# Taking gathered picks 24 at a time in a tuned two-layer expert kernel

## The chip, the cores and the metric

One core of a Trainium2 chip. The metric is device time in microseconds (us) of one launch; 2041.65 us is the median of three runs before the change (2041.55 to 2047.14).

## The reference

A backbone of two layers for 256 latent and 256 context tokens of width 1024, all in fp32. Layer 1 mixes with state-space heads and latent attention, layer 2 with a chunked gMLP. Each layer ends in a PEER expert block, where the change does most of its work:

```python
s1 = jnp.einsum('thd,hkd->thk', q[..., :half], k1)
s2 = jnp.einsum('thd,hkd->thk', q[..., half:], k2)
v1, i1 = lax.top_k(s1, PEER_TOPK)
v2, i2 = lax.top_k(s2, PEER_TOPK)
...
top_s, j = lax.top_k(cand_s, PEER_TOPK)
idx = jnp.take_along_axis(cand_i, j, axis=-1)
gate = jax.nn.softmax(top_s.astype(jnp.float32), axis=-1).astype(h.dtype)
...
act = jax.nn.gelu(jnp.einsum('phkd,pd->phk', jnp.take(u_tab, ib, axis=0), tb), approximate=False)
return jnp.einsum('phk,phkd->pd', gb * act, jnp.take(v_tab, ib, axis=0))
```

So each of the 256 tokens picks 8 heads × 16 = 128 of 16384 experts, each with a gate; an expert is a row of `u_tab`, against which the token is scored, and a row of `v_tab`, which is added with gate × gelu(score). Every sub-layer is scaled and shifted by a modulation vector, the product of a condition with `ada_w` (1024 × 6144 per layer).

## The kernel before

Every instruction is issued through a wrapper, so nearly all carry the line of that helper, L169 (L173 in the changed kernel), and are told apart by their tiles. The wrapper also books the instruction in a planner (`Clock`) that keeps a planned time per engine. `schedule()` takes several generators and goes on with the one whose engine is least far; a generator yields conditions on the planned times. The order of each engine's queue is fixed so, when the program is built; on the chip each engine runs its queue in order and waits on semaphores.

The expert block, `peer()`, works on two tiles of 128 tokens. A pick's expert number is class × 128 + row. The first X = 75 classes are computed densely, the picks of all others are gathered.

- `stage2(t)` finds the 128 picks of each token and writes the sort key `key[t]`, for gathered picks only, and the gates `gte[t]`.
- First pass: 75 "S units", each of 8 matmuls `pa<-phf,wr` (128x256), for one class, its 512 KB of weights loaded on the SP queue into one of 4 buffers `wr`. `spread()` turns the dense picks' gates into columns by matmuls `pb<-oc,o`, whose operands the vector engine (DVE) builds.
- Second pass: 75 "V units", each of 8 matmuls `pb<-wr,ge`, again 512 KB a unit.
- Beside both passes `gather()` handles the picks of the other classes, one per token at a time. `take8()` takes the eight largest keys of every token: it unpacks the row and the place among the 128 picks, and fetches the gate at that place by eight multiplies `mk` over 128 columns. `fetch()` on POOL loads 128 rows of 8 KB (u and v together) by an indirect DMA into one of NR = 6 buffers `rows`. On DVE `dot()` writes `junk` and the score, and `accumulate()` adds into `acc`.
- Each tile of tokens has CAP = 56 picks of its own gathered so. The up to LEFT = 16 others of a token go to three shared lists of 128. `listing()` counts them (`cnt`, a flag `fl`) on DVE, ranks them by small matmuls on the tensor engine (PE) (`pa<-cnt,tri`, `pa<-cnt,ones`, `pa<-fl,ones`), then by comparisons `cmp` and matmuls `pa<-rhs,cmp`. The lists are fetched (`rows<-in_uv,lidx` with their tokens' vectors `rows<-hs,lidx`) and added by matmuls `pb<-rows,sc` of 512 columns into the second pass's sums.
- `ending()` takes tile 0's `acc` through DRAM (`acs`, written and read on the SP queue, where the weight loads stand too) and adds the input of the layer.
- `overflow()` is a branch for more left-over picks than the lists hold.

The modulation is made by `ada_group()`: pieces of 128 × 512 of `ada_w` come on the SP queue into NAW = 4 buffers `aw`, one matmul `pb<-aw,condT` with 32 output rows each. Its generator runs beside the other work of the hybrid layer.

Of the kernel before, what the change touches and what calls it, by code (L numbers as in the profile page):

```python
# [10 lines left out]
F32 = mybir.dt.float32  # L11
# [3 lines left out]
I32 = mybir.dt.int32  # L15
# [5 lines left out]
P = 128  # L21
# [6 lines left out]
GSC = 32768.0  # L28
ROOM = 36
TB, TL = 8, 4  # L30
CAP = 56
ROUNDS = 9
SHARED = 3
# [16 lines left out]
NAW = 4  # L50
KORDER = (8, 10, 12, 0, 2, 4, 6, 14)
LAG = 2

# [144 lines left out]
def tile_backbone(ctx: ExitStack, tc: tile.TileContext, a: dict, out: bass.AP):  # L198
# [50 lines left out]

    def mm(o, lhsT, rhs, start=True, stop=True):  # L250
        T.matmul(o, lhsT, rhs, start=start, stop=stop)

# [48 lines left out]
    ms = [dp.tile([P, 512], F32, name=f"ms{g}") for g in (1, 2)]  # L301
    LEFT = 8 * ROUNDS - CAP
    lts = dp.tile([2 * P * LEFT, 2], F32, name="lts")

# [1108 lines left out]
    def peer(l, mod, a2, sh2):  # L1413
# [3 lines left out]

        key = [[q1.tile([P, P], F32, name=f"key{t}{i}") for i in range(2)] for t in range(2)]
        iota_i = key[0][0].bitcast(I32)
        G.iota(iota_i, [[1, P]], base=0, channel_multiplier=0)  # L1420
        jp1 = q1.tile([P, P], F32, name="jp1")
        V.tensor_scalar(jp1, iota_i, 1.0, None, op0=ALU.add)
        place_i = q1.tile([P, SHARED], I32, name="place_i")
# [14 lines left out]
        pkT = [q1.tile([P, 4, P], F16, name=f"pkT{t}") for t in range(2)]  # L1438
        gidx = [q1.tile([P, 8 * ROUNDS], I32, name=f"gidx{t}") for t in range(2)]
        gsel = [q1.tile([P, 8 * ROUNDS], F32, name=f"gsel{t}") for t in range(2)]  # L1440
        gte = [q1.tile([P, P], F32, name=f"gte{t}") for t in range(2)]
# [47 lines left out]
        def stage2(t):  # L1489
# [107 lines left out]

        def take8(t, r_, idx=None, gsl=None):

            if idx is None:  # L1600
                idx, gsl = gidx[t][:, 8 * r_:8 * r_ + 8], gsel[t][:, 8 * r_:8 * r_ + 8]
# [3 lines left out]
            ki = q2.tile([P, 8], I32, tag="ki", name="ki")  # L1605
            V.tensor_copy(ki, ks)
            z_ = q2.tile([P, 8], F32, tag="z_", name="z_")
            V.tensor_scalar(z_, ks, 0.0, 65536.0, op0=ALU.is_equal, op1=ALU.mult)
            V.tensor_scalar(idx, ki, 8, None, op0=ALU.logical_shift_right)
            V.tensor_tensor(idx, idx, z_, op=ALU.add)  # L1610
            V.tensor_scalar(ki, ki, 255, None, op0=ALU.bitwise_and)
            j1 = q2.tile([P, 8], F32, tag="j1", name="j1")
            V.tensor_copy(j1, ki)
# [146 lines left out]
        def choose():  # L1760
            wait[0], feed.eager = QWAIT, False
            yield lambda: "q" in done
            wait[0] = GTH
            yield from stage2(0)
            for i, _ in enumerate(stage2(1)):
                if i == 4:
                    turn(0)
                yield
            for r_ in range(EARLY):
                take8(0, r_)  # L1770
# [12 lines left out]
            done.add("G")  # L1783
            todo_v[:] = []
            wait[0] = LAST
# [23 lines left out]
        def listing():  # L1809

            ps = pa()
            rhs = q2.tile([P, 2, 2], F32, tag="rhs", name="rhs", bufs=1)
            V.memset(rhs, 1.0)
            for t in range(2):
                vm = q2.tile([P, LEFT], F32, tag="vm", name="vm")
# [7 lines left out]
                fl = q2.tile([P, 1], F32, tag="fl", name="fl")  # L1823
                V.tensor_reduce(fl, key[t][ROUNDS % 2], axis=AX.X, op=ALU.max)
                V.tensor_scalar(fl, fl, 0.0, None, op0=ALU.is_gt)
                mm(ps[:, t:t + 1], tri, cnt[:, t:t + 1], True, t == 0)
# [3 lines left out]
                mm(ps[:, 3 + 2 * t:4 + 2 * t], ones, fl)  # L1830
# [3 lines left out]
            V.tensor_tensor(ends[:, 2:4], ends[:, 2:4], ps[:, 4:6], op=ALU.add)  # L1834
            ps = pa()
# [26 lines left out]
        def gather():  # L1862
# [7 lines left out]
            def issue():  # L1870
# [4 lines left out]
                if t < 2:  # L1875
                    if s % 8 == 0 and s // 8 >= taken[t]:
                        take8(t, taken[t])
                        taken[t] += 1
# [42 lines left out]
            while work or pend:  # L1921
                weigh_last()
                if work:
# [6 lines left out]
                    if t == 1 and s >= 4:  # L1930

                        if taken[0] < ROUNDS or taken[1] < ROUNDS:
                            t_ = 0 if taken[0] < ROUNDS else 1
                            take8(t_, taken[t_])
                            taken[t_] += 1
                        elif lst is None:
                            lst = listing()
                        if lst:
                            next(lst, None)
                if len(pend) > LAG or not work:  # L1940
                    if len(pend) == 1:
                        weigh_last()
                    if pend[0][0] == 2:
                        yield at(pend[0][3])
                    accumulate()
                while head[0] < len(todo) and len(work) + len(pend) < NR:
                    if todo[head[0]][0] == 2 and todo[head[0]][1] == 0:
                        while taken[0] < ROUNDS or taken[1] < ROUNDS:
                            t_ = 0 if taken[0] < ROUNDS else 1
                            take8(t_, taken[t_])  # L1950
                            taken[t_] += 1
# [34 lines left out]
        def overflow():  # L1986
# [8 lines left out]
            with tc.If(rv > 0):  # L1995
                for t in range(2):
# [3 lines left out]
                    V.tensor_tensor(gsel[t][:, CAP:], gsel[t][:, CAP:], pos, op=ALU.mult)  # L2000
                    for r_ in range(CAP // 8, P // 8):
                        if r_ < ROUNDS:
                            idx, gsl = gidx[t][:, 8 * r_:8 * r_ + 8], gsel[t][:, 8 * r_:8 * r_ + 8]
                        else:
                            idx = q2.tile([P, 8], I32, tag="oidx", name="oidx")
                            gsl = q2.tile([P, 8], F32, tag="ogs", name="ogs")
                            take8(t, r_, idx, gsl)
                        for s in range(max(0, CAP - 8 * r_), 8):
                            rw = qr["rows"][s % NR]
# [121 lines left out]
```

## Time and profile before

| | us |
|---|---|
| median of three runs | 2041.65 |
| the profiled execution | 2042.83 |
| its span in the profile | 2041.0 |
| busy: tensor engine / its weight loads | 1886.9 / 1516.0 |
| busy: vector engine | 1429.6 |
| busy: scalar engine / GpSimd | 545.9 / 630.8 |

The profile is of one execution. PE is the tensor engine, PEld its weight loads, DVE the vector engine, ACT the scalar engine, POOL GpSimd, SP the queue on which the weights are loaded. Matmuls are pipelined and their ends modelled; an fp32 matmul of 128x256 leaves two records, so a unit of 8 leaves 16. A timeline row groups like instructions in a row and gives in brackets the idle time before the first of them and what ended it. 1.8 us of the execution's time lie outside the span.

### The profile page before, as it was taken

How to read it: one execution, taken by the hardware profiler on the slowest of the kernel's cores; microseconds unless marked ns; L12 is line 12 of the kernel's file. 1: busy time of each engine (PE TensorE's matmuls, PEld its weight loads, DVE VectorE, ACT ScalarE, POOL GpSimd, SP SyncE). 2: the span in 40 equal slices, each digit the busy share in tenths (PEclk: the TensorE clock that was granted, in tenths of full speed). 3: DMA queues.
4: the chain of work that ended last, by engine and by line, in shares of the span. 5: the costliest groups of instructions: out<-in, count | busy, mean ns of one | idle time of the engine just before them, and what ended most of it. 6: DMA issues, size and time to landing. Idle time of an engine off the chain costs nothing.

```text
span 2041.0 us, 28033 instructions
## 1 busy us (share of the span) xinstructions
PE 1886.9 (92%) x9728; PEld 1516.0 (74%) x9728; DVE 1429.6 (70%) x3796; ACT 545.9 (27%) x1438; POOL 630.8 (31%) x402
## 2 busy tenths in 40 slices
PE   7899999999989999987999798999899999978997
PEld 3666444479968888876878588789778888867785
DVE  3565576246996888879767526478988888697665
ACT  4434253354212222110111254443122221101111
POOL 2324312176011112232422279551112112224221
PEclk9999999999989999999899899999989999988999
DMA  8555664545366889998899464453578888988993
GB/s 298 181 172 200 225 222 138 190 160 187 129 225 241 286 306 336 351 377 313 316 417 394 175 227 164 140 192 127 188 295 294 325 324 319 366 316 318 417 402 132
DMA packets 133065, 529.87 MB, mean 260 GB/s; under 512 B 17941, under 2 KB 18133, under 8 KB 105197
## 3 DMA queue, kind: packets, MB, share of 16 engines
q1 hardware_dynamic: 97440, 301.76, 41.8%
q0 software_dynamic: 34176, 225.07, 29.1%
q8 instruction: 77, 1.26, 0.3%
q10 hardware_dynamic: 1296, 1.16, 0.2%
q14 instruction: 76, 0.62, 0.1%
HBM read 540.28 MB, written 6.91 MB: 268 GB/s over the span
## 4 chain that ended last, share of the span: by engine, by line
PE 36%; issue 29%; DVE 17%; POOL 12%; ACT 2%; DMA 2%; POOLq 0%; SPq 0%; ACTq 0%; DVEq 0%
PE pa L169 23%; PE pb L169 14%; POOL rows L169 10%; DVE ge L169 6%; POOL whl L169 2%; DVE rows L169 1%; DVE acc L169 1%; DMA rows<-hs,lidx 1%; DVE oc L169 1%; DVE junk L169 1%; DVE mk L169 1%; DVE x L169 1%; DVE o L169 1%; DVE cacc L169 0%; POOLq L169 0%
## 5 line engine op out<-in xcount | busy, mean ns | idle before, releaser
L169 POOL DMA_INDIRECT rows<-in_uv,gidx x224 | 266.8, 1191 | 930.0 <-DVE acc L169 619.9
L169 PE MATMUL pb<-wr,ge 128*128 128x256 f32 x2400 | 542.1, 386 | 13.1 <-DMA wr<-in_dn 11.3
L169 PE MATMUL pa<-phf,wr 128*128 128x256 f32 x2400 | 539.8, 385 | 0.0
L169 PEld LDWEIGHTS pb<-wr,ge 128*128 128x128 f32 x2400 | 458.5, 193 | 96.5 <-DMA wr<-in_dn 32.1
L169 PEld LDWEIGHTS pa<-phf,wr 128*128 128x128 f32 x2400 | 459.8, 193 | 62.0
L169 POOL TENSOR_TENSOR whl<-wr,whl 128x1024 fp32r<-128x1024 f32 (+2 forms) x130 | 314.7, 2434 | 363.6 <-ACT whl L169 337.4
L169 DVE SCALAR_TENSOR_TENSOR junk<-rows,h 128x1024 bf16<-128x1024 f32 x224 | 273.5, 1221 | 99.9 <-DMA rows<-in_uv,gidx 99.7
L169 DVE SCALAR_TENSOR_TENSOR acc<-rows,wt,acc 128x1024 f32<-128x1024 f32 x220 | 281.8, 1281 | 0.0
L169 ACT ACTIVATE act<-act 128x1 f32<-128x1 f32 x230 | 47.0, 204 | 547.3 <-DVE junk L169 531.8
L169 ACT CAST whl<-wr 128x1024 fp32r<-128x1024 f32 (+2 forms) x136 | 136.9, 1019 | 74.5 <-issue 26.4
L169 ACT ACTIVATE sg<-pa 128x256 f32<-128x256 f32 (+25 forms) x116 | 34.4, 296 | 352.4 <-PE pa L169 313.1
L169 PE MATMUL pb<-oc,o 128*128 128x75 f16 x1024 | 85.3, 252 | 28.6 <-DVE oc L169 26.8
L169 PEld LDWEIGHTS <-o 128*128 128x128 f16 x1024 | 78.2, 118 | 38.0 <-DVE o L169 16.5
L169 PE MATMUL pa<-phh,whl 128*128 128x256 f32 x512 | 96.3, 285 | 2.6 <-DVE phf L169 2.2
L169 PE MATMUL pb<-aw,condT 128*32 128x512 f32 x328 | 94.0, 624 | 3.5 <-DVE mod L169 2.7
L169 DVE SCALAR_TENSOR_TENSOR ge<-pb,ge 128x80 f32<-128x80 f32 (+31 forms) x128 | 37.0, 323 | 73.4 <-ACT ge L169 73.2
L169 PEld LDWEIGHTS pa<-phh,whl 128*128 128x128 f32 x512 | 80.8, 191 | 4.7 <-DVE phf L169 2.5
L169 DVE SCALAR_TENSOR_TENSOR mk<-jp,j,gte 128x128 f32<-128x128 f32 x288 | 81.5, 348 | 1.3
L169 PE MATMUL pa<-phl,whl 128*128 128x256 f32 x256 | 73.2, 286 | 2.3 <-POOL phl L169 1.3
L169 ACT ACTIVATE wt<-act,gsel 128x1 f32<-128x1 f32 x224 | 66.0, 295 | 7.3
L169 PE MATMUL pb<-whl,cath 128*128 128x512 f32 x192 | 61.8, 400 | 2.0 <-POOL whl L169 1.2
L169 ACT ACTIVATE ge<-pa 128x256 f32<-128x256 f32 (+24 forms) x136 | 40.2, 296 | 81.4 <-PE pa L169 81.4
(525 smaller groups left out, 2436.2 us busy)
## 6 DMA issues: line engine op xcount, KB each, us to landing
wr<-in_dn SPq DMA_DIRECT2D x300, 512.0 KB, 6.6
aw<-in_ada_w SPq DMA_DIRECT2D x164, 256.0 KB, 3.3
wr<-in_wq SPq DMA_DIRECT2D x32, 512.0 KB, 3.2
wr<-in_w_out SPq DMA_DIRECT2D x16, 512.0 KB, 3.3
wr<-in_gm_w_v SPq DMA_DIRECT2D x16, 512.0 KB, 3.6
wr<-in_gm_w_u SPq DMA_DIRECT2D x16, 512.0 KB, 3.4
wr<-in_gm_w_out SPq DMA_DIRECT2D x16, 512.0 KB, 3.2
wr<-in_w_xbc SPq DMA_DIRECT2D x12, 512.0 KB, 4.8
```

The source lines that it names most:

```text
L169: return f(*args, **kw)
```

## The change

Five edits.

1. `take8` becomes `take`: 24 picks at a time, three takes a tile in place of nine. The gate is no longer looked up: `stage2` makes three keys per tile (5 more operations of 128x128, and 2 products with the mask), all with the place `jd` in their high bits, and the row, the gate's upper and its lower part below. Three MAX8 and three MATCH_REPLACE8 per eight picks sort all three alike. Of the takes before the spread (EARLY) one is left in place of two. The picks now come in the order of their place, not of their expert number.
2. `listing()` does its DVE work first, yields four times, and only then issues its counting matmuls; the comparisons are made at once, and the `rhs,cmp` matmuls follow three yields later.
3. The `sc` matmuls are issued LATE = 6.0 planned us behind the point where their weights are ready.
4. `mm()` issues an fp32 matmul of 512 columns and 128 output rows as two of 256 columns (92 of them in the order).
5. `ada_group()` handles its pieces in pairs: it waits for two, issues their matmuls, and then two loads.

```diff
-ROOM = 36
+ROOM = 38
...
-ROUNDS = 9
+TAKE, TAKES = 24, 3
...
+LATE = 6.0
...
     def mm(o, lhsT, rhs, start=True, stop=True):
+        if rhs.dtype == F32 and lhsT.dtype == F32 and len(rhs.shape) == 2 and rhs.shape[1] == 512 and o.shape[0] == P:
+
+            T.matmul(o[:, :256], lhsT, rhs[:, :256], start=start, stop=False)
+            T.matmul(o[:, 256:], lhsT, rhs[:, 256:], start=False, stop=stop)
+            return
         T.matmul(o, lhsT, rhs, start=start, stop=stop)
...
-        for i in range(len(units) + n - 1):
+        for i in range(0, len(units) + n, 2):
+            if i >= n:
+
+                yield at(*bufs[i % n:i % n + 2])
+                for j in range(2):
+                    k, t = units[i - n + j]
+                    mm(ps[32 * t:32 * t + 32, :], condT[:, k, :], bufs[i % n + j], k == 0, k == KD - 1)
             if i < len(units):
-                k, t = units[i]
-                aw = bufs[i % n]
-                yield lambda: clk["T"] >= clock.idle(aw)
-                Q.dma_start(out=aw, in_=a["ada_w"][l, k * P:(k + 1) * P, g * 2048 + t * 512:g * 2048 + (t + 1) * 512])
-            if i >= n - 1:
-                k, t = units[i - n + 1]
-                aw = bufs[(i - n + 1) % n]
-                yield at(aw)
-                mm(ps[32 * t:32 * t + 32, :], condT[:, k, :], aw, k == 0, k == KD - 1)
+                yield lambda: clk["T"] >= max(clock.idle(x) for x in bufs[i % n:i % n + 2])
+                for j in range(2):
+                    k, t = units[i + j]
+                    Q.dma_start(out=bufs[i % n + j], in_=a["ada_w"][l, k * P:(k + 1) * P, g * 2048 + t * 512:g * 2048 + (t + 1) * 512])
...
-            V.scalar_tensor_tensor(key[t][0], cg, 256.0, jp1, op0=ALU.mult, op1=ALU.add)
+            V.scalar_tensor_tensor(key[t][0], jd, float(ROWS), cg, op0=ALU.mult, op1=ALU.add)
             V.tensor_tensor(key[t][0], key[t][0], mk, op=ALU.mult)
+            yield
+
+            gi = qr["s"].tile([P, P], I32, tag="gi", name="gi")
+            V.tensor_scalar(gi, gte[t], GHI, None, op0=ALU.mult)
+            V.scalar_tensor_tensor(cg, gte[t], GHI, gi, op0=ALU.mult, op1=ALU.subtract)
+            V.scalar_tensor_tensor(key[t][1], jd, 65536.0, gi, op0=ALU.mult, op1=ALU.add)
+            V.tensor_scalar(gi, cg, GLO, 32768.0, op0=ALU.mult, op1=ALU.add)
+            V.scalar_tensor_tensor(key[t][2], jd, 65536.0, gi, op0=ALU.mult, op1=ALU.add)
+            for i in (1, 2):
+                V.tensor_tensor(key[t][i], key[t][i], mk, op=ALU.mult)
...
-        EARLY = 2
+        EARLY = 1
...
-        def take8(t, r_, idx=None, gsl=None):
+        def take(t, r_, idx=None, gsl=None):
...
-            ks = q2.tile([P, 8], F32, tag="ks", name="ks")
-            V.max(ks, key[t][r_ % 2])
-            V.match_replace(key[t][(r_ + 1) % 2], ks, key[t][r_ % 2], 0.0)
...
-            for s_ in range(8):
-                mk = q2.tile([P, P], F32, tag="mk", name="mk")
-                V.scalar_tensor_tensor(mk, jp1, j1[:, s_:s_ + 1], gte[t], op0=ALU.is_equal, op1=ALU.mult, accum_out=gsl[:, s_:s_ + 1])
+            ks = [tmp(f"ks{i}", F32) for i in range(3)]
+            for e in range(0, TAKE, 8):
+                for i in range(3):
+                    V.max(ks[i][:, e:e + 8], key[t][i])
+                for i in range(3):
+                    V.match_replace(key[t][i], ks[i][:, e:e + 8], key[t][i], 0.0)
...
+            V.tensor_scalar(lo, kc, 1.0 / (GLO * GHI), -32768.0 / (GLO * GHI), op0=ALU.mult, op1=ALU.add)
+            V.scalar_tensor_tensor(gsl, kb, 1.0 / GHI, lo, op0=ALU.mult, op1=ALU.add)
+            V.tensor_tensor(gsl, gsl, ok, op=ALU.mult)
...
+            for _ in range(4):
+                yield
+            ps = pa()
+            for t in range(2):
                 mm(ps[:, t:t + 1], tri, cnt[:, t:t + 1], True, t == 0)
...
+            for _ in range(3):
+                yield
             ps = pa()
             for k in range(SHARED):
                 for t in range(2):
-                    cmp = q2.tile([P, P], F32, tag="cmp", name="cmp", bufs=4)
-                    V.tensor_scalar(cmp, iotaL[:, :P], float(k * P), ends[:, t:t + 1], op0=ALU.add, op1=ALU.is_ge)
-                    mm(ps[:, 2 * k:2 * k + 2], cmp, rhs[:, t, :], t == 0, t == 1)
+                    mm(ps[:, 2 * k:2 * k + 2], cmps[2 * k + t], rhs[:, t, :], t == 0, t == 1)
...
                     if pend[0][0] == 2:
-                        yield at(pend[0][3])
+                        yield lambda: clk["T"] >= clock.ready(pend[0][3]) + LATE
                     accumulate()
```

How the change moves instructions, at three places. First PE's queue in the second pass of layer 1, around the listing and up to the first `sc` matmuls; a unit is 8 of the `pb<-wr,ge` matmuls, and 128 of these stand ahead of the rows shown, with one modulation row (136 with the change). Before:

```order
L169 MATMUL pb<-wr,ge 128x256 x120
L169 MATMUL pa<-cnt,tri 128x1
L169 MATMUL pa<-cnt,ones 128x1
L169 MATMUL pa<-fl,ones 128x1
L169 MATMUL pa<-cnt,tri 128x1
L169 MATMUL pa<-cnt,ones 128x1 x2
L169 MATMUL pa<-fl,ones 128x1
L169 MATMUL pb<-wr,ge 128x256 x8
L169 MATMUL pa<-rhs,cmp 128x2 x6
L169 MATMUL pb<-wr,ge 128x256 x320
L169 MATMUL pb<-rows_4515,sc 128x512 x4
```

With the change:

```order
L173 MATMUL pb<-wr,ge 128x256 x56
L173 MATMUL pa<-cnt,tri 128x1
L173 MATMUL pa<-cnt,ones 128x1
L173 MATMUL pa<-fl,ones 128x1
L173 MATMUL pa<-cnt,tri 128x1
L173 MATMUL pa<-cnt,ones 128x1 x2
L173 MATMUL pa<-fl,ones 128x1
L173 MATMUL pb<-wr,ge 128x256 x24
L173 MATMUL pa<-rhs,cmp 128x2 x6
L173 MATMUL pb<-wr,ge 128x256 x344
L173 MATMUL pb<-rows_4581,sc 128x256 x8
```

The counting matmuls stand behind 24 units where they stood behind 31 (128 and 120 matmuls; now 136 and 56), `rhs,cmp` behind 27 in place of 32, and the `sc` matmuls behind 70 and 71 in place of 72. In layer 2 it is 24 for 30, 28 for 30, and 70 and 71 for 71.

The second is DVE's queue ahead of the listing in layer 1. Before, the last take of eight, an accumulate, a dot and the first row of the listing; ten such takes, one after each dot, stand in a row here:

```order
L169 MAX ks<-key_3250 128x8
L169 MATCH_REPLACE key_3251<-ks,key_3250 128x128
L169 CAST ki<-ks 128x8
L169 TENSOR_SCALAR z__7676<-ks 128x8
L169 TENSOR_SCALAR gidx_3273<-ki 128x8
L169 TENSOR_TENSOR gidx_3273<-gidx_3273,z__7676 128x8
L169 TENSOR_SCALAR ki<-ki 128x8
L169 CAST j_7681<-ki 128x8
L169 SCALAR_TENSOR_TENSOR mk,gsel_3275<-jp_3253,j_7681,gte_3277 128x128 x8
L169 SCALAR_TENSOR_TENSOR acc<-rows_4511,wt,acc 128x1024
L169 SCALAR_TENSOR_TENSOR junk,act<-rows_4514,h_3265 128x1024
L169 MEMSET rhs 128x4
```

With the change, the end of the last take and what follows it:

```order
L173 TENSOR_SCALAR lo<-kc 128x24
L173 SCALAR_TENSOR_TENSOR gsel_3331<-kb,lo 128x24
L173 TENSOR_TENSOR gsel_3331<-gsel_3331,ok 128x24
L173 SCALAR_TENSOR_TENSOR acc<-rows_4582,wt,acc 128x1024
L173 SCALAR_TENSOR_TENSOR junk,act<-rows_4579,h_3321 128x1024
L173 MEMSET rhs 128x4
L173 TENSOR_SCALAR vm<-gidx_3328 128x16
L173 TENSOR_REDUCE cnt<-vm 128x1
```

What a dot waits behind is now one take of 24 for each of three dots: one soon after the start of the pass, two right ahead of the listing. 45 of a layer-1 tile pair's 112 own gathers were issued before the second pass, now 49; in layer 2 it was 48 and is 49. Ahead of the listing stand, from the pass's start, 29 gathers in layer 1 before and 22 now (26 and 22 in layer 2), with 12 takes of eight before and 3 of 24 now in either.

The third is the SP queue around `acs` in layer 1. Before:

```order
L169 DMA wr<-in_dn 128x1024 x94
L169 DMA acs<-acc 128x1024
L169 DMA ge<-xs_89 128x1024
L169 DMA ge<-xs_90 128x1024
L169 DMA ge<-acs 128x1024
L169 DMA wr<-in_dn 128x1024 x56
```

With the change:

```order
L173 DMA wr<-in_dn 128x1024 x92
L173 DMA acs<-acc 128x1024
L173 DMA wr<-in_dn 128x1024 x3
L173 DMA ge<-xs_89 128x1024
L173 DMA ge<-xs_90 128x1024
L173 DMA ge<-acs 128x1024
L173 DMA wr<-in_dn 128x1024 x55
```

Three weight loads now stand between the write of `acs` and its read, as they do in layer 2 before. In layer 2 with the change four loads stand between them, behind the two `xs` loads.

The modulation matmuls `pb<-aw,condT` number 164 in both orders of PE. They stand in 82 runs before (27 of one, 39 of two, 5 of three, 11 of four) and in 69 with the change (1, 54, 1, 13). One unit more of the first pass stands ahead of the first spread matmul in both layers.

## Rows read from the trace of the kernel before

**Rows 1.** The page, busy time of the engines.

```profile
PE 1886.9 (92%) x9728; PEld 1516.0 (74%) x9728; DVE 1429.6 (70%) x3796; ACT 545.9 (27%) x1438; POOL 630.8 (31%) x402
```

**Rows 2.** What PE waits for, whole span: us in total, times, longest us.

```profile
PE pa L169 <- DVE cnt L169: 28.0, 2, 14.3
PE pb L169 <- DVE oc L169: 26.8, 11, 8.8
...
PE pb L169 <- DMA wr<-in_dn: 11.3, 5, 7.1
```

**Rows 3.** PE's timeline, layer 1: start, us, group, [idle before <- releaser].

```profile
841.11 55.51 PE L169 MATMUL pb<-wr,ge 128*128 128x256 f32 x256
...
915.30 43.82 PE L169 MATMUL pb<-wr,ge 128*128 128x256 f32 x192 [7.07 <-DMA wr<-in_dn]
972.82 0.56 PE L169 MATMUL pa<-cnt,tri 128*128 128x1 f32 x2 [13.69 <-DVE cnt L169]
...
975.79 6.29 PE L169 MATMUL pb<-wr,ge 128*128 128x256 f32 x16
...
983.18 144.57 PE L169 MATMUL pb<-wr,ge 128*128 128x256 f32 x640
1137.25 12.71 PE L169 MATMUL pb<-rows,sc 128*128 128x512 f32 x24 [9.50 <-DVE sc L169]
```

**Rows 4.** PE's timeline, layer 2.

```profile
1794.11 34.37 PE L169 MATMUL pb<-wr,ge 128*128 128x256 f32 x144 [3.22 <-DMA wr<-in_dn]
1842.80 0.56 PE L169 MATMUL pa<-cnt,tri 128*128 128x1 f32 x2 [14.32 <-DVE cnt L169]
...
1849.97 33.74 PE L169 MATMUL pb<-wr,ge 128*128 128x256 f32 x144
...
2004.13 8.83 PE L169 MATMUL pb<-rows,sc 128*128 128x512 f32 x16 [2.18 <-DVE sc L169]
```

**Rows 5.** Windows: us, busy per engine, PE clock, DMA share, GB/s.

```profile
974.00:978.00 4.00, 4.00 (x15) 3.62 (x15) 3.96 (x9) 0.57 (x3) 1.73 (x1) 0.50 0.77 258
...
1020.00:1071.00 51.00, 50.34 (x220) 40.32 (x219) 32.02 (x40) 6.47 (x26) 13.46 (x14) 1.00 1.02 417
```

**Rows 6.** DVE's timeline, one take of eight between two gathers, layer 1.

```profile
912.07 1.22 DVE L169 SCALAR_TENSOR_TENSOR junk<-rows,h 128x1024 bf16<-128x1024 f32 x1
...
913.22 0.29 DVE L169 MAX8 ks<-key 128x8 f32<-128x128 f32 x1
...
914.85 0.35 DVE L169 SCALAR_TENSOR_TENSOR mk<-jp,j,gte 128x128 f32<-128x128 f32 x1
...
917.04 1.29 DVE L169 SCALAR_TENSOR_TENSOR acc<-rows,wt,acc 128x1024 f32<-128x1024 f32 x1
```

**Rows 7.** DVE's groups by form: busy us, mean ns of one, idle before.

```profile
L169 DVE MAX8 ks<-key 128x8 f32<-128x128 f32 x36 | 10.4, 289 | 0.1
...
L169 DVE MATCH_REPLACE8 key<-ks,key 128x128 f32<-128x128 f32 x36 | 9.9, 276 | 0.0
...
L169 DVE CAST j<-ki 128x8 f32<-128x8 int32 x36 | 6.2, 172 | 1.2
...
L169 DVE TENSOR_TENSOR key<-key,ge 128x128 f32<-128x128 f32 x4 | 1.2, 292 | 0.1
```

**Rows 8.** POOL's timeline, layer 1: issue of the first shared list.

```profile
1123.09 1.89 POOL L169 DMA_INDIRECT rows<-in_uv,lidx  x1 [1.83 <-DVE acc L169]
```

**Rows 9.** PE's timeline, hybrid layer: two runs of modulation matmuls.

```profile
82.93 1.05 PE L169 MATMUL pb<-aw,condT 128*32 128x512 f32 x2
...
84.39 1.05 PE L169 MATMUL pb<-aw,condT 128*32 128x512 f32 x4
```

**Rows 10.** PE's timeline, hybrid layer: two 512-column matmuls.

```profile
275.59 1.02 PE L169 MATMUL pa<-hc,bcT 128*128 128x512 f32 x2
276.45 1.02 PE L169 MATMUL pb<-hs,bcT 128*128 128x512 f32 x2
```

**Rows 11.** What PE's weight loads wait for: us in total, times, longest us.

```profile
PEld pb L169 <- DMA aw<-in_ada_w: 6.2, 11, 1.2
```

More of the change, by code (lines that the diff above doesn't have):

```diff
@@ L1416, in peer @@
         q2 = es.enter_context(tc.tile_pool(name="q2", bufs=2))
-        key = [[q1.tile([P, P], F32, name=f"key{t}{i}") for i in range(2)] for t in range(2)]
+        key = [[q1.tile([P, P], F32, name=f"key{t}{i}") for i in range(3)] for t in range(2)]
         iota_i = key[0][0].bitcast(I32)
         G.iota(iota_i, [[1, P]], base=0, channel_multiplier=0)
-        jp1 = q1.tile([P, P], F32, name="jp1")
-        V.tensor_scalar(jp1, iota_i, 1.0, None, op0=ALU.add)
+        jd = q1.tile([P, P], F32, name="jd")
+        V.tensor_scalar(jd, iota_i, -1.0, float(P), op0=ALU.mult, op1=ALU.add)
         place_i = q1.tile([P, SHARED], I32, name="place_i")
@@ L1438, in peer @@
         pkT = [q1.tile([P, 4, P], F16, name=f"pkT{t}") for t in range(2)]
-        gidx = [q1.tile([P, 8 * ROUNDS], I32, name=f"gidx{t}") for t in range(2)]
-        gsel = [q1.tile([P, 8 * ROUNDS], F32, name=f"gsel{t}") for t in range(2)]
+        gidx = [q1.tile([P, TAKE * TAKES], I32, name=f"gidx{t}") for t in range(2)]
+        gsel = [q1.tile([P, TAKE * TAKES], F32, name=f"gsel{t}") for t in range(2)]
         gte = [q1.tile([P, P], F32, name=f"gte{t}") for t in range(2)]
@@ new lines, in take @@
+                idx, gsl = (x[t][:, TAKE * r_:TAKE * (r_ + 1)] for x in (gidx, gsel))
+            tmp = lambda n, dt: q2.tile([P, TAKE], dt, tag=n, name=n)
+            ks = [tmp(f"ks{i}", F32) for i in range(3)]
[4 more added lines that the diff above has]
+                    V.match_replace(key[t][i], ks[i][:, e:e + 8], key[t][i], 0.0)
+            ki, kb, kc = (tmp(f"k{n}", I32) for n in "ibc")
@@ new lines, in take @@
+            for k_, x in ((ki, ks[0]), (kb, ks[1]), (kc, ks[2])):
+                V.tensor_copy(k_, x)
+            z_, ok, lo = (tmp(n, F32) for n in ("z_", "ok", "lo"))
+            V.tensor_scalar(z_, ks[0], 0.0, 65536.0, op0=ALU.is_equal, op1=ALU.mult)
+            V.tensor_scalar(ok, ks[0], 0.0, None, op0=ALU.is_gt)
+            V.tensor_scalar(idx, ki, ROWS - 1, None, op0=ALU.bitwise_and)
+            V.tensor_tensor(idx, idx, z_, op=ALU.add)
+            V.tensor_scalar(kb, kb, 65535, None, op0=ALU.bitwise_and)
@@ L1769, in choose @@
             for r_ in range(EARLY):
-                take8(0, r_)
+                take(0, r_)
                 yield
@@ L1829, in listing @@
                 mm(ps[:, 2 + 2 * t:3 + 2 * t], ones, cnt[:, t:t + 1])
[L1830 removed]
+                mm(ps[:, 3 + 2 * t:4 + 2 * t], ones, fls[t])
             yield
@@ L1834, in listing @@
             V.tensor_tensor(ends[:, 2:4], ends[:, 2:4], ps[:, 4:6], op=ALU.add)
+            cmps = []
+            for k in range(SHARED):
+                for t in range(2):
+                    cmp = q2.tile([P, P], F32, tag="cmp", name="cmp", bufs=2 * SHARED)
+                    V.tensor_scalar(cmp, iotaL[:, :P], float(k * P), ends[:, t:t + 1], op0=ALU.add, op1=ALU.is_ge)
+                    cmps.append(cmp)
+            for _ in range(3):
+                yield
             ps = pa()
@@ L1875, in issue @@
                 if t < 2:
-                    if s % 8 == 0 and s // 8 >= taken[t]:
-                        take8(t, taken[t])
+                    if s % TAKE == 0 and s // TAKE >= taken[t]:
+                        take(t, taken[t])
                         taken[t] += 1
@@ L1930, in gather @@
                     if t == 1 and s >= 4:
-                        if taken[0] < ROUNDS or taken[1] < ROUNDS:
-                            t_ = 0 if taken[0] < ROUNDS else 1
-                            take8(t_, taken[t_])
+                        if taken[0] < TAKES or taken[1] < TAKES:
+                            t_ = 0 if taken[0] < TAKES else 1
+                            take(t_, taken[t_])
                             taken[t_] += 1
@@ L1947, in gather @@
                     if todo[head[0]][0] == 2 and todo[head[0]][1] == 0:
-                        while taken[0] < ROUNDS or taken[1] < ROUNDS:
-                            t_ = 0 if taken[0] < ROUNDS else 1
-                            take8(t_, taken[t_])
+                        while taken[0] < TAKES or taken[1] < TAKES:
+                            t_ = 0 if taken[0] < TAKES else 1
+                            take(t_, taken[t_])
                             taken[t_] += 1
@@ L2000, in overflow @@
                     V.tensor_tensor(gsel[t][:, CAP:], gsel[t][:, CAP:], pos, op=ALU.mult)
-                    for r_ in range(CAP // 8, P // 8):
-                        if r_ < ROUNDS:
-                            idx, gsl = gidx[t][:, 8 * r_:8 * r_ + 8], gsel[t][:, 8 * r_:8 * r_ + 8]
-                        else:
[L2005 to L2008, printed above, removed]
+                    for r_ in range(CAP // TAKE, -(-P // TAKE)):
+                        if r_ < TAKES:
+                            idx, gsl = (x[t][:, TAKE * r_:TAKE * (r_ + 1)] for x in (gidx, gsel))
+                        else:
+                            idx = q2.tile([P, TAKE], I32, tag="oidx", name="oidx")
+                            gsl = q2.tile([P, TAKE], F32, tag="ogs", name="ogs")
+                            take(t, r_, idx, gsl)
+                        for s in range(max(0, CAP - TAKE * r_), TAKE):
                             rw = qr["rows"][s % NR]
```

20 lines of the change are left out of this document (8 added, 12 removed).

## The prediction

> **What bounds the kernel now.** I read the page's busy times first: the tensor engine is busy for 92% of the span, the vector engine for 70% [rows 1]. The time is therefore the tensor engine's own work and its stalls, and of the new code only what alters one of these counts. Next I read what the tensor engine waits for [rows 2]: three of the longest belong to the expert layers, `cnt` (28.0 us in 2), `oc` (26.8 in 11, the longest 8.8) and the weight stream (11.3 in 5). Then I read the engine's timeline over the second pass of layer 1 [rows 3] and of layer 2 [rows 4], to see which unit each stall stands before. One unit of that pass is 8 matmuls, 16 records; 256 records in 55.5 us make 3.47 us per unit, and 640 in 144.6 make 3.61.
>
> In layer 1 the engine stands 13.69 us for `cnt`; in layer 2 14.32 us [rows 3, 4]. The vector timeline says why: each eight picks there cost, from the MAX8 at 913.22 to the next accumulate at 917.04, 3.82 us, of which eight `mk` multiplies (914.85 to 917.04) are 2.19 [rows 6]. The listing must wait for all picks; in the old order ten such takes stand in a row among the gathers. The wait has a tail: behind it the granted clock is 0.50, its lower level of 1.2 GHz, after the engine had stood nearly idle [rows 5]; the listing takes 2.97 us (972.82 to 975.79), and the unit behind it 6.29, or 6.1 without the modelled end of its last matmul, instead of 3.47 [rows 3].
>
> **The change part by part.** The sum is made against the profiled execution: span 2041.0, its time 2042.83, which is 1.18 above the median of 2041.65. A measurement of this kernel tells about 0.3% from no change, 6 us.
>
> *Price of a take.* The new one has 9 MAX8 (289 ns), 9 MATCH_REPLACE8 (276) and 12 small operations like the cast (172) [rows 7]: 7.2 us of busy time. Operations overlap: the `mk` ones, 0.35 us each, come 0.27 apart [rows 6]. By that ratio 7.2 becomes 5.6; with the small value loads 6.1 is my estimate (bounds 5 and 8). Three old takes are 11.5. The seven key operations per tile (292 ns at most [rows 7]) add 1.6.
>
> *Listing.* The change puts its matmuls after 24 units in both layers, instead of 31 and 30, so the tensor engine asks 7 × 3.47 = 24.3 and 20.8 us earlier. Does the vector engine come sooner by more? After the pass's start it has 3 takes instead of 12: 45.8 − 18.3 = 27.5 us saved. Also 7 gathers fewer stand ahead in layer 1 and 4 in layer 2, because 4 and 1 more are issued before the pass (counted in the two orders); at 2.35 us each (a dot from 912.07 to 913.22, an accumulate of 1.29 less its overlap [rows 6]) that is 16.5 and 9.4. Layer 1: 27.5 + 16.5 − 24.3 − 13.7 = 6 us early; layer 2: 27.5 + 9.4 − 20.8 − 14.3 = 2 us early. Both waits go, narrowly. With them go half of the listing's 2.97 (1.5, at twice the clock) and the slow unit's excess (2.7). So 13.69 + 4.2 and 14.32 + 4.2 are 36.4; I leave 2 per layer for the thin margin: **−33** (bounds −36 and −15, the latter with 10 us left in each). The `rhs` matmuls come 3 or 4 units later with their comparisons already made, so they wait for nothing.
>
> *Wait for weights.* The 7.07 us before 915.30 in layer 1 are weight loads queued on SP behind the read of `acs` that waits for its own write. In the new order three loads go between write and read, which is layer 2's old order, whose wait is 3.22 [rows 3, 4]. Layer 1: −4; layer 2 gets a fourth load: −1. **−5** (−10 to 0).
>
> *The end of the pass.* Its `sc` matmuls need the last shared gather, whose descriptors POOL issues at 1123.09, 14.2 us before 1137.25 [rows 3, 8]. Taking the stall out brings the tensor engine there sooner, but not the bytes. Up to that issue layer 1 moves about 70 weight units of 0.524 MB and 67 gathers of 1.05 MB, 107 MB in 282 us, 379 GB/s; now 63 gathers, 103 MB. The busiest stretch shows 417 GB/s with the DMA engines' share at 1.02 [rows 5]. At 417 the `sc` matmuls can start 247 + 14 = 261 us after the pass's start, at the old mean 271 + 14 = 285. The tensor engine alone would be there at 70 × 3.47 + 9 for modulation, listing, `rhs` and what is left of the wait for weights = 252. I take 270, nearer the first, since the stall that lowered the old mean is cut short. So 18 us per layer go to stretched units and the `sc` wait. Now it is 40 × 0.14 + 9.5 = 15 in layer 1, and 12 in layer 2: from 1849.97 to 2004.13 stand 41 units, 142 us at 3.47, in 154 [rows 4]. **+9** (−9 to +39). The matmuls now come with two other units among them, which moves their wait and not the last byte. The Trainium skill's page "Perfetto Trace Analysis", section Roofline, says that a core working alone is bounded by its 16 DMA engines at some 435 GB/s; by that rule the bytes would allow 237 + 14 = 251 us, the tensor engine alone would set the end, and the time would come some 36 us lower (an estimate). The trace shows no stretch of this pass above 417.
>
> *Start of the spread.* The old wait there is 8.8 at most [rows 2]. The vector engine does one new take instead of two old ones (6.1 against 7.6) and both tiles' keys (3.2): it is about 2 us later. The tensor engine has one more unit of work (3.5) ahead of it: **−2** over both layers (±4). Beside the rest of the first pass stand two new takes where four old ones stood (12.2 for 15.3), so nothing is added there.
>
> *Modulation matmuls in pairs.* A run of them costs 1.05 us whether it has two records or four, one matmul or two [rows 9]. The order has 82 runs before (27 single) and 69 after (1 single): 13 × 1.0. Half of it lies where the engine waits for others anyway, and the planner reorders what stands around: **−7** (−15 to +8). The Trainium skill's page "TensorEngine Tiling (Array Packing)", section Key Properties, says that changing the tiling mode drains the engine while the tiles of a mode work independently; by that rule alone all 13 us would come, and the rows, with 1.05 for one and two, agree with it.
>
> *Halves.* A 512-column matmul follows the next by 0.86 us [rows 10]; four records of 256 columns, at 3.47/16, make 0.87. 92 of them: **+1** (0 to +5).
>
> Sum, in this order: −33 − 5 + 9 − 2 − 7 + 1 = −37; 2042.8 − 37 = 2005.8, less the 1.18 about **2004** as a median. Nothing is charged for the larger code at the end, which lies in a branch that isn't taken.
>
> **The rivals.** *1. The wait moves to the shared lists.* The gathers are bound by bytes and not by picks, and the mean stays at 379 GB/s: 15 us more per layer than I took, 285 for 270, so about **2034**. For it: the share of 1.02 in the long stretch [rows 5], and that 9.5 us were lost there already [rows 3]. Against it: 417 has been reached.
>
> *2. The listing is still late.* If a take costs 9 us rather than 6, 3 × 3 us eat layer 1's margin of 6 and layer 2's of 2: 3 + 7 us of wait, and the slow clock behind it (8.4) back, some **2022**, less what the bytes would have cost anyway.
>
> *3. Slower: pairs that wait.* The new `ada_group` waits for two landed pieces before either matmul, and issues the next two only then; four buffers no longer keep three loads in flight. Today 11 waits on such a piece come to 6.2 us, the longest 1.2 [rows 11]. In 69 runs, 1.2 each would be +83 on 2004 + 7, for **2094**; it ends slower than before (2048) from a mean of (2048 − 2011)/69 = 0.54 us per run. Against it: the waits now average 0.56 and only 11 pieces have one.
>
> *4. Better.* Bytes flow at 417 throughout (261 for 270, −18), and the pairs bring all 13 (−6): **1980**.
>
> **How the numbers follow.** The forecast, 1985 to 2020, has 0.57; rival 1 (2020 to 2036) 0.22; rival 2 0.06; rival 3 0.06; rival 4 0.06; 0.03 is left for a change that in the hybrid layer's reordering gives back what it gains. The range 1978 to 2032 takes in the forecast's bounds and most of rivals 1, 2 and 4; above it lies rival 1's upper end. Faster by over 0.3% are the forecast, rivals 1, 2 and 4 less a little: 0.88; within 0.3% 0.06; slower 0.06.
>
> **What would show it.** Right: no wait for `cnt` over 3 us in the list of the tensor engine's waits and a clock of 1.00 around the listing; the takes some 6 us long; 3 us before the unit that follows the `acs` read; `sc` waits of 7 to 15 per layer; the second pass of layer 1 near 300 us instead of 319. Wrong: a `cnt` wait of over 5; `sc` waits of over 20 (rival 1); waits on `aw` over 20 us in sum (rival 3); a change in the stretch before the expert layers of more than 15 us either way.

## The result, and the profile after

The changed kernel takes 1992.83 us (median of four runs, 1991.93 to 1993.09); the kernel before took 2041.6 beside it. The ratio is 0.9756 (95% interval 0.9737 to 0.9775): faster by 48.8 us, where 2004 and a range of 1978 to 2032 had been forecast. The profiled execution took 1993.09 us, its span 1991.3 instead of 2041.0.

Where the time went is read first from the starts of the stages on the tensor engine, each the first such matmul in its timeline:

| first matmul of | before, us | after, us | gained up to there |
|---|---|---|---|
| layer 1's output projection, `pb<-whl,cath` | 408.8 | 396.5 | 12.3 |
| layer 1's first pass, `pa<-phf,wr` | 522.3 | 512.1 | 10.2 |
| layer 1's second pass, `pb<-wr,ge` | 841.1 | 829.4 | 11.7 |
| layer 2's gated mixing, `pa<-whl,ghh` | 1173.8 | 1141.1 | 32.7 |
| layer 2's second pass | 1716.7 | 1679.5 | 37.2 |
| end of the span | 2041.0 | 1991.3 | 49.7 |

So 12 us come from what stands ahead of layer 1's second pass, nearly all of them from the hybrid mixing, 21 from that pass, 4.5 from layer 2's mixing and first pass, 12.5 from its second pass and the tail.

The waits of the tensor engine after the change, as in [rows 2]:

```profile
PE pb L173 <- DVE oc L173: 24.5, 13, 7.6
PE pb L173 <- DVE sc L173: 24.1, 2, 14.8
...
PE pb L173 <- DMA wr<-in_dn: 8.0, 7, 2.6
```

The wait for `cnt`, 28.0 us before, is gone from the list; `sc` has taken its place, with twice the 12.2 that it had before:

```profile
PE pb L169 <- DVE sc L169: 12.2, 3, 9.5
```

The timeline of layer 1's second pass shows the listing without a wait and the new wait, to be read against [rows 3]:

```profile
829.40 55.64 PE L173 MATMUL pb<-wr,ge 128*128 128x256 f32 x256
...
892.83 10.63 PE L173 MATMUL pb<-wr,ge 128*128 128x256 f32 x48 [2.65 <-DMA wr<-in_dn]
905.29 14.08 PE L173 MATMUL pb<-wr,ge 128*128 128x256 f32 x64 [1.84 <-DMA wr<-in_dn]
919.21 0.28 PE L173 MATMUL pa<-cnt,tri 128*128 128x1 f32 x2
...
920.69 10.61 PE L173 MATMUL pb<-wr,ge 128*128 128x256 f32 x48
...
1096.94 9.94 PE L173 MATMUL pb<-rows,sc 128*128 128x256 f32 x32 [9.37 <-DVE sc L173]
```

The listing now takes 1.48 us (919.21 to 920.69) where it took 2.97, since its small matmuls run at the higher clock, 0.28 us for the first where [rows 3] has 0.56. The granted clock there is 1.00, where [rows 5] has 0.50:

```profile
919.00:921.00 2.00, 2.00 (x18) 1.95 (x17) 2.00 (x4) 0.28 (x2) 1.37 (x1) 1.00 1.03 428
```

The three units behind it take 3.5 us each, where the one behind it took 6.3. In layer 2 the `cnt` row has no wait either, but the wait for `sc` is longer:

```profile
1747.97 17.53 PE L173 MATMUL pb<-wr,ge 128*128 128x256 f32 x80 [1.48 <-DMA wr<-in_dn]
1765.34 0.28 PE L173 MATMUL pa<-cnt,tri 128*128 128x1 f32 x2
...
1950.92 9.62 PE L173 MATMUL pb<-rows,sc 128*128 128x256 f32 x32 [14.76 <-DVE sc L173]
```

The two stretches from the start of the pass to the `sc` matmuls, and layer 1's up to the issue of the first shared list, as windows with the columns of [rows 5]:

```profile
829.40:1082.90 253.50, 246.77 (x1135) 210.31 (x1134) 178.78 (x361) 33.47 (x133) 81.44 (x67) 1.00 0.97 386
829.40:1096.90 267.50, 251.44 (x1155) 214.09 (x1153) 188.66 (x374) 35.45 (x141) 86.20 (x72) 0.99 0.97 385
1679.50:1950.90 271.40, 252.52 (x1155) 213.94 (x1153) 191.97 (x396) 35.84 (x143) 87.75 (x72) 0.98 0.97 383
```

The DMA engines are busy for 0.97 of them, at 383 to 386 GB/s. That issue, to be read against [rows 8], comes 14.0 us ahead of the `sc` matmuls, as it did before (14.2):

```profile
1082.95 0.99 POOL L173 DMA_INDIRECT rows<-in_uv,lidx  x1 [0.62 <-DVE acc L173]
```

The vector engine's timeline shows a take of 24 in place of three like [rows 6]:

```profile
901.28 0.68 DVE L173 MAX8 ks<-key 128x8 f32<-128x128 f32 x3
...
906.79 0.18 DVE L173 TENSOR_TENSOR gsel<-gsel,ok 128x24 f32<-128x24 f32 x1
906.89 1.28 DVE L173 SCALAR_TENSOR_TENSOR acc<-rows,wt,acc 128x1024 f32<-128x1024 f32 x1
...
911.21 0.15 DVE L173 TENSOR_SCALAR fl<-fl 128x1 f32<-128x1 f32 x1
```

It takes 5.61 us (901.28 to 906.89), and the listing's last flag is ready 8 us before its matmuls are reached. Last, the group of the modulation matmuls by line, before and after, and what the weight loads now wait for there, to be read against [rows 11]:

```profile
L169 PE MATMUL pb<-aw,condT 128*32 128x512 f32 x328 | 94.0, 624 | 3.5 <-DVE mod L169 2.7 <-DMA aw<-in_ada_w 0.7
...
L173 PE MATMUL pb<-aw,condT 128*32 128x512 f32 x328 | 78.9, 618 | 1.0 <-DVE mod L173 0.7 <-DMA aw<-in_ada_w 0.3
...
PEld pb L173 <- DMA aw<-in_ada_w: 2.7, 5, 1.2
```

The 328 records took 94.0 us before and take 78.9 now.

### The profile page after: what moved, and what is told of

It is laid out like the page before. It is cut to its first block, busy times and chain, and to the rows that moved or that the text cites. A ratio compares the mean times of both kernels' runs of the same rounds, so it can differ in the third digit from the quotient of the medians.

```text
span 1991.3 us, 28013 instructions
## 1 busy us (share of the span) xinstructions
PE 1858.1 (93%) x9909; PEld 1539.8 (77%) x9909; DVE 1375.9 (69%) x3391; ACT 546.0 (27%) x1430; POOL 630.5 (32%) x401
## 4 chain that ended last, share of the span: by engine, by line
PE 45%; issue 22%; DVE 17%; POOL 10%; DMA 3%; ACT 2%; POOLq 0%; ACTq 0%; DVEq 0%; SPq 0%
PE pa L173 30%; PE pb L173 15%; POOL rows L173 8%; DVE ge L173 6%; POOL whl L173 2%; DMA rows<-in_uv,gidx 2%; DVE rows L173 1%; DVE key L173 1%; DVE seg L173 1%; DMA rows<-hs,lidx 1%; DVE acc L173 1%; DVE x L173 1%; DVE ks L173 1%; DVE cacc L173 0%; DVE oc L173 0%
## 5 line engine op out<-in xcount | busy, mean ns | idle before, releaser
L173 PE MATMUL pb<-wr,ge 128*128 128x256 f32 x2400 | 532.1, 381 | 9.5 <-DMA wr<-in_dn 8.0
L173 PEld LDWEIGHTS pb<-wr,ge 128*128 128x128 f32 x2400 | 451.4, 190 | 87.6 <-DMA wr<-in_dn 27.5
L173 ACT ACTIVATE sg<-pa 128x256 f32<-128x256 f32 (+22 forms) x114 | 34.3, 301 | 343.6 <-PE pa L173 312.3
L173 PE MATMUL pb<-oc,o 128*128 128x75 f16 x1024 | 85.2, 252 | 25.5 <-DVE oc L173 24.5
L173 DVE SCALAR_TENSOR_TENSOR ge<-pb,ge 128x108 f32<-128x108 f32 (+24 forms) x128 | 36.4, 320 | 64.3 <-ACT ge L173 64.2
L173 PE MATMUL pb<-aw,condT 128*32 128x512 f32 x328 | 78.9, 618 | 1.0 <-DVE mod L173 0.7
L173 ACT ACTIVATE ge<-pa 128x256 f32<-128x256 f32 (+21 forms) x130 | 38.7, 299 | 84.5 <-PE pa L173 84.5
L173 DVE TENSOR_TENSOR oc<-eq,pkT 128x600 f16<-128x600 f16 x128 | 54.6, 468 | 2.2
L173 DVE MAX8 ge<-ge 128x8 f32<-128x128 f32 (+1 forms) x192 | 38.4, 255 | 24.8 <-ACT ge L173 24.7
```

Of the source, the lines that this page charges most:

```text
L173: return f(*args, **kw)
```

## The experiments

Times are medians of four runs; the kernel before, run beside them, took 2043.5 to 2045.7, which is 2 to 4 us above its first median, so differences of less than 4 us decide nothing. The ratio is to the kernel before, with its 95% interval.

**1. Modulation pieces one by one again.** The generator of the kernel before, in the changed kernel.

```diff
-        for i in range(0, len(units) + n, 2):
+        for i in range(len(units) + n - 1):
...
+                mm(ps[32 * t:32 * t + 32, :], condT[:, k, :], aw, k == 0, k == KD - 1)
```

> The changed kernel with the modulation pieces handled one by one again, as before the change. The changed kernel runs in 1992.8 us. Theory: of the 49 us gained, 12 lie ahead of the output projection of layer 1 (its first matmul came at 408.8 us and now comes at 396.5), and the pairs brought them, at some 1 us for each of the 13 runs saved: this kernel then takes 2002 to 2006 us and its output projection starts at 405 us or later. Rival: the halved 512-column matmuls brought them, whose weight loads no longer wait: this kernel then stays within 4 us of 1993.

2002.12 us, ratio 0.9802 (0.9762 to 0.9842). Layer 1's output projection starts at 407.4 us instead of 396.5, and the group is back at its old cost:

```profile
L173 PE MATMUL pb<-aw,condT 128*32 128x512 f32 x328 | 94.6, 629 | 4.3 <-DVE mod L173 3.1 <-DMA aw<-in_ada_w 1.1
```

The theory held: the pairs bring some 9 us of the total and 11 up to the output projection. The matmuls' own busy time fell by 15.7 (94.6 to 78.9); the rest of that is given back around them.

**2. 512-column matmuls whole again.**

```diff
-        if rhs.dtype == F32 and lhsT.dtype == F32 and len(rhs.shape) == 2 and rhs.shape[1] == 512 and o.shape[0] == P:
...
-            return
         T.matmul(o, lhsT, rhs, start=start, stop=stop)
```

> The changed kernel with the 512-column fp32 matmuls issued whole again. Theory: two halves cost what the whole costs (0.87 against 0.86 us), so within 4 us of 1993. Rival (the halves brought the 12 us ahead of the output projection of layer 1): 2001 to 2006 us.

1988.82 us, ratio 0.9743 (0.9703 to 0.9782): 4.2 us below 1993, at the edge of the theory's 4, and far from the rival. The output projection starts 1.6 us earlier than with halves, at 394.9. The halves gain nothing here; that they cost a microsecond or two is not shown, since other runs with halves start it anywhere from 395.1 (experiment 6) to 397.3 (experiment 3).

**3. The old listing with the new takes.**

```diff
-            for _ in range(4):
-                yield
             ps = pa()
...
-            for _ in range(3):
-                yield
```

> The changed kernel with the old listing, whose counting matmuls are asked for as soon as the vector engine is told to count: behind 20 and 21 units of the second pass in place of 24, with the takes of 24 kept. From the changed kernel's trace the vector engine's last flag came 8 us ahead of the first counting matmul in layer 1 and at the same time in layer 2; asked for 13.9 and 10.4 us sooner, the tensor engine waits some 5 us for cnt in layer 1 and 10 in layer 2, and the listing and the unit behind it run at the lower clock (4 us each). Theory (the end of the pass is set by the bytes of the gathers): the waits for sc, 9.4 and 14.8 us, shrink by as much, and the time is 1995 to 2001. Rival (the terms add): 2011 to 2018 us.

2004.34 us, ratio 0.9814 (0.9776 to 0.9853), between the two. The waits for `cnt` are about what was expected, 7.5 and 8.9 us for 5 and 10, and most of what they cost came off the waits for `sc`:

```profile
PE pa L173 <- DVE cnt L173: 16.4, 2, 8.9
...
PE pb L173 <- DVE sc L173: 10.2, 2, 6.5
```

`sc` fell from 24.1 to 10.2 us, by 13.9 where `cnt` rose by 16.4. The first `sc` matmul came 273.4 and 276.5 us after the start of its pass, 5.9 and 5.0 later than in the changed kernel. Its timeline shows what a stall at the listing costs besides:

```profile
910.22 0.56 PE L173 MATMUL pa<-cnt,tri 128*128 128x1 f32 x2 [7.54 <-DVE cnt L173]
...
913.20 6.10 PE L173 MATMUL pb<-wr,ge 128*128 128x256 f32 x16
```

A wait of 7.54 us brings the slow listing (2.98 us, at a granted clock of 0.50) and the slow unit back, some 4 us in this layer and 3 in the other. With them the sum is 16.4 + 7 − 13.9, some 10 of the 11.5 us by which this kernel is slower. Neither theory alone is right: a stall ahead delays the pass's end, but by less than the stall.

**4. The `sc` matmuls much later.**

```diff
-LATE = 6.0
+LATE = 24.0
```

> The changed kernel with LATE at 24 instead of 6 planned us: the sc matmuls stand behind 73 and 75 units in place of 70 and 71, so that three or four units more hide the last gathers' arrival. Theory: the waits for sc (9.4 and 14.8 us) fall to under 1 and to 1 to 5, the sum of the rest stays, so 1970 to 1977 us. Rival: the units that were behind the sc matmuls now take the bytes from the lists, or the wait moves to the end of the layer, where nothing stands behind it: 1988 to 1994 us.

1970.39 us, ratio 0.9643 (0.9607 to 0.9679), as the theory had it. There is no wait for `sc` at all:

```profile
1100.51 3.62 PE L173 MATMUL pb<-rows,sc 128*128 128x256 f32 x16
1103.96 7.07 PE L173 MATMUL pb<-wr,ge 128*128 128x256 f32 x32
1110.87 7.07 PE L173 MATMUL pb<-rows,sc 128*128 128x256 f32 x32
```

In layer 1 they start 270.6 us after the pass's start and in layer 2 268.0, about when they did in the changed kernel (267.5 and 271.5), but the engine has spent the wait on units that stood behind them. This version beats both kernels.

**5. The new listing with the old takes**, in the kernel before.

```diff
+            for _ in range(4):
+                yield
             ps = pa()
...
+            for _ in range(3):
+                yield
```

> The kernel before with the new listing alone: old takes of eight, but the counting matmuls four yields later (behind 35 units instead of 31 and 30) and their comparisons made ahead. It takes 13.9 and 17.4 us of waiting from the tensor engine at the counting, which is all of the 13.7 and 14.3 that it waits for cnt there. Theory (the picks and the bytes of the gathers set when the shared lists arrive, and neither is touched): the waits for sc, 9.5 and 2.2 us before, grow by most of what was saved, and the time is 2026 to 2037 us. Rival (the stall at the counting was the cost, and moving the matmuls would have done without the new takes): 2003 to 2012 us.

2027.39 us, ratio 0.9920 (0.9888 to 0.9951), in the theory's band, but only in part by its mechanism. No wait for `cnt` remains, and others grew:

```profile
PE pb L169 <- DMA wr<-in_dn: 19.0, 5, 10.2
PE pb L169 <- DVE sc L169: 16.1, 2, 8.4
```

Of the 28 us of `cnt`, 12 came back as these two, more of it for weights (11.3 to 19.0) than for `sc` (12.2 to 16.1), which was to take most. The `sc` matmuls came 289.3 and 288.9 us after the start, where the kernel before had 296.1 and 287.4. To bring them to 270 it takes the edit of the takes. No run separates what is in that edit: shorter takes, one early take in place of two, fewer gathers left for the pass, and picks in another order.

**6. Half the weight bytes of the second pass.** From the fifth class on, half of each v weight is left out of the computation; matmuls and gathers are as many.

```diff
+        feed.short |= {len(feed.srcs) + i for i, (w, c_) in enumerate(PEER) if w == "V" and c_ >= 4}
...
+                m_ = kk * n // 2 if self.n in self.short else kk * n
-                Q.dma_start(out=raw[:, :kk * n], in_=src.rearrange("p k n -> p (k n)"))
+                Q.dma_start(out=raw[:, :m_], in_=src.rearrange("p k n -> p (k n)")[:, :m_])
...
-                                mm(py[t][n // 2][:, n % 2 * 256:(n % 2 + 1) * 256], g_[:, t * P:(t + 1) * P], v_[:, 2 * n:2 * n + 2, :],
+                                mm(py[t][n // 2][:, n % 2 * 256:(n % 2 + 1) * 256], g_[:, t * P:(t + 1) * P], v_[:, 2 * (n % 2):2 * (n % 2) + 2, :],
```

> The changed kernel with half the weight bytes in the second pass: of each class from the fifth on only the first 256 KB are loaded, and all its matmuls read that half, so the second half of the v weights is left out of the computation. Gathers, takes and matmul counts stay. Theory (bytes): with about 84 MB instead of 103 up to the shared lists the waits for sc (9.4 and 14.8 us) fall under 2 us each, the second passes' units come back to 3.47 us, and the time is 1955 to 1968 us. Rival (the chain of 63 gathers through six buffers, with its dots and accumulates, sets the arrival whatever the bytes): the waits for sc stay above 6 us each and the time above 1980 us.

1941.73 us, ratio 0.9495 (0.9466 to 0.9524), faster than either theory. One wait for `sc` is left, and the units between are back at 656/16 = 41 in 141.8 us, 3.46 each:

```profile
925.76 141.83 PE L173 MATMUL pb<-wr,ge 128*128 128x256 f32 x656
1069.88 8.86 PE L173 MATMUL pb<-rows,sc 128*128 128x256 f32 x32 [2.29 <-DVE sc L173]
```

The rival falls: as many gathers through the same six buffers arrive in time when the weights leave them bytes. The first shared list is issued 226.8 and 227.4 us after the start of its pass, instead of 253.6 and 260.3 (in layer 1 the `sc` matmuls stand behind 68 units here). The expected gain was too small: the two second passes with their tails gave back 47 us together, of which the waits for `sc` are 22.

**7. LATE 24 and whole matmuls together.** The edits of 4 and 2.

> The changed kernel with LATE at 24 and the 512-column matmuls issued whole: the two edits that came out best so far together (1970.4 and 1988.8 us, against 1992.8). Theory: they add, since one is ahead of the second passes and the other at their end: 1964 to 1970 us. Rival (the 4 us of the whole matmuls were chance): 1969 to 1973 us.

1969.57 us, ratio 0.9642 (0.9610 to 0.9674): not distinguishable from run 4, and in the bands of both expectations. Of the 4 us of run 2 less than one is left here, so they were mostly chance or do not add.

**8. No take ahead of the spread.** On top of run 7.

```diff
-        EARLY = 1
+        EARLY = 0
```

> The kernel of LATE 24 and whole matmuls, with no take ahead of the spread (EARLY 0 in place of 1): the first take stands behind the spread's first block on the vector engine. A take measured 5.6 us; the tensor engine waits 7.6 us for the first oc in layer 1. Theory: that wait falls to about 2 us in both layers, but the take now delays the spread's second block, for which the tensor engine has units of the first pass to do: 8 to 11 us faster than without, 1955 to 1961 us. Rival: the wait only moves to the second block: within 3 us of the kernel of LATE 24 and whole matmuls.

1987.77 us, ratio 0.9718 (0.9688 to 0.9748): 18 us slower than run 7, and both expectations fall. In its timeline the wait is split in two:

```profile
589.74 0.23 PE L173 MATMUL pb<-oc,o 128*128 128x75 f16 x1 [1.35 <-DVE oc L173]
...
597.21 0.23 PE L173 MATMUL pb<-oc,o 128*128 128x75 f16 x1 [5.84 <-DVE oc L173]
```

There was no unit to do between the first two blocks, and a wait of 5.3 us for `ge` came in the same pass. The loss lies in the first passes: from the start of the first to that of the second it is 328.2 us in layer 1 and 329.8 in layer 2, where run 7 has 317.5 and 318.1. Waits explain some 6 us of that in layer 1. The granted clock from 560 to 600 us was 0.83 instead of 0.87, run 7 first:

```profile
560.00:600.00 40.00, 31.87 (x167) 27.64 (x166) 36.68 (x100) 4.62 (x16) 8.45 (x6) 0.87 0.66 240
...
560.00:600.00 40.00, 27.14 (x135) 22.89 (x134) 36.58 (x99) 4.05 (x14) 3.56 (x3) 0.83 0.33 107
```

What took the rest wasn't traced.

**9. No LATE.**

```diff
-                        yield lambda: clk["T"] >= clock.ready(pend[0][3]) + LATE
+                        yield at(pend[0][3])
```

> The changed kernel without LATE: the sc matmuls are issued as soon as the planner holds their weights ready, all three lists together behind 70 units in both layers, in place of 70, 70 and 71. Theory: half a unit does not matter beside waits of 9.4 and 14.8 us, since the bytes of the last gather set the start: within 4 us of the changed kernel's 1992.8. Rival (with all three together the third list's arrival is waited for as well, without the unit that stood ahead of it): 1997 to 2002 us.

1993.28 us, ratio 0.9759 (0.9742 to 0.9775), and 23.1 us of waits for `sc`: the third of the five edits, as the change has it, does nothing that these runs can tell.

**10. The first spread block later.** On top of run 4.

```diff
-                    pend.append((t, b, scored[0], o1, oc, clk["V"]))
+                    pend.append((t, b, scored[0], o1, oc, clk["V"] + (0.0 if t or b else 8.0)))
```

> The kernel of LATE 24 (1970.4 us) with the first block of the spread issued 8 planned us later on the tensor engine, nothing moved on the vector engine: some two more units of the first pass stand ahead of it. Theory: the wait for the first oc (7.6 us in layer 1, as much in layer 2) falls under 2 us in each, and with it the clock's fall behind it: 1953 to 1960 us. Rival (the blocks behind the first one become as late as the first was early, as without the early take): 1967 to 1974 us.

1972.19 us, ratio 0.9645 (0.9625 to 0.9665): no gain, and the first wait is unmoved.

```profile
596.15 1.63 PE L173 MATMUL pb<-oc,o 128*128 128x75 f16 x16 [7.62 <-DVE oc L173]
```

The edit didn't do what it was meant to: the first block still stands behind 22 units of the first pass, as in run 4, because a unit that is scored after the spread began waits for it, and the generator stops after three of these. The question was not answered by this run. That the time is unmoved hides two changes: layer 1's second pass took 295.0 us in place of 303.4, with 50 gathers issued in the first pass in place of 48, and layer 2's first pass took 326.0 in place of 318.3.

## Why the prediction was right

The direction, the largest term and the range held; the gain was 49 us where 37 were worked out.

**Listing** (−33; the text's own figures give 36.4 less 4, which is 32.4). Right in mechanism and size. The waits of 28.0 us are gone, the listing gained 1.5 us in each layer, and the slow units are gone in both. The margins were worked out at 6 and 2 us; measured, the last flag came 8 us ahead in layer 1, and in layer 2 just as the matmuls were reached. The 2 us per layer left in for it weren't needed. The `rhs` matmuls, which were to wait for nothing, still wait 1.35 us in layer 2 (1.50 before). The price of a take, 6.1 us by estimate, measured 5.6: the busy time scaled by the overlap of the `mk` operations gave it exactly, and the addition for the value loads was too much. Experiment 5 adds what the text didn't say: moving the listing alone would have brought some 16 to 18 of the 49 us.

**Wait for weights** (−5). 7.07 fell to 2.65 and then 1.84 in front of the next group, 3.22 to 1.48: −4.3. Over the whole span such waits fell by 3.3 (11.3 to 8.0).

**End of the pass** (+9). The mechanism held, and the number held best: the `sc` matmuls were put at 270 us after the start of each pass and came at 267.5 and 271.5. Against the 252 put down for the tensor engine alone that is 35 us lost, where 36 were taken. Experiment 6 shows that these are bytes: with half the weights' bytes, waits and stretched units both go.

That the number held so well is in part luck. The 270 was placed by judgement between 261 and 285, and both of its factors were off: 103 MB up to the issue in 256 us would be 402 GB/s, while the trace has 386 GB/s for 253.5 us, which is 97.8 MB. Fewer bytes made up for the lower rate. The issue at 1123.09 is also that of the first shared list, as [rows 8] says, and not of the last, as the text has it; it is the first that the `sc` matmuls wait for. And the 252 was some 5 too high: in experiment 6 layer 2's `sc` matmuls came, without a wait, 247 us after the start behind as many units.

The Trainium skill's page "Perfetto Trace Analysis", section Roofline, gives some 435 GB/s as the most that one core's DMA engines move; at that rate the tensor engine alone would have set the end. As a ceiling the runs do not contradict it, but this mix of loads and gathers stayed below it: 385 GB/s over the whole stretch at a share of 0.97, and 418 over the 50 us from 971. Before the change the highest was no lower, 418 over the 50 us from 1003, where the text has no stretch above 417.

**Start of the spread** (−2). The working held: counted from the pass's start, layer 1's first spread matmul came 1.6 us later (84.3 for 82.7), behind 22 units in place of 21. The longest wait fell from 8.8 to 7.6 and the sum from 26.8 to 24.5. By the text's own figures, 3.5 less 2 in each layer, the term should have been −3. From the first pass's start to the second's the gain is 1.5 us in layer 1 and 3.8 in layer 2, over twice the estimate; but experiment 5, which leaves the spread as it was, shows 1.6 and 0.5 there, so layer 1's part is no sign of the term.

**Pairs** (−7). The mis-sized term. The 13 runs saved were taken at half their 13 us, since the engine waits for others there. Measured, the output projection came 12.3 us earlier, 10.2 were left at the first pass, and experiment 1 gives 9.3 in the total. Halving it had no row behind it. Of the rival of pairs that wait nothing is seen: waits on `aw` fell from 6.2 to 2.7 us among the weight loads.

**Halves** (+1). Experiment 2 does not contradict it, within what it can tell.

The span fell by 12.7 us more than the sum of −37. By place, some 4 of them lie ahead of layer 1's first pass (10.2 us gained for the 6 of pairs and halves), 4 in its second pass (21 gained where −17 was worked out, from −17.9 + 2 − 4 + 3), 4 in the two first passes and layer 2's mixing, and 1 in layer 2's second pass. The first rival, `sc` at 285 us, had the right place and too high a price; the second and third did not occur.

## What to carry to other kernels

Where an order written ahead makes an engine ask too early, compare what it waits for with what stands behind the wait in its queue: the units behind the `sc` matmuls could run by then, and putting them in front (experiment 4) brought 22 us without making anything faster. A wait removed upstream of a saturated transfer comes back partly at that transfer, so work out the arrival by bytes first and put it beside the engine's own time. And ask of each bundled edit what it does alone: of the five here the pairs (9 us), the listing (11 to 18) and, by what is left, the takes carry the gain, while LATE at 6 and the halves carry none that the runs can tell.

## What had not been expected

Three independent MAX8 in a row took 0.68 us together (the row at 901.28), where one alone is given 0.29 [rows 6]: they follow each other by 0.2 us. And taking a take away ahead of the spread made the kernel 18 us slower (experiment 8), although the engine that it freed was the one waited for.
